# Hybrid decoder block: where the first tokens' last transposes of h stand, and what the second tokens' updates queue behind

## The chip, the cores and the metric

The kernel runs on one core of a Trainium2 chip. The metric is the time of one execution in microseconds (us) of device time, the median of several runs. The core has five engines that run side by side: TensorE (PE) for matmuls, VectorE (DVE) and ScalarE (ACT) for elementwise work, GpSimd (POOL), and SyncE (SP), which here issues the DMAs. Each engine runs its own list of instructions in order. Where an instruction needs what another engine makes, it waits for a semaphore. PE writes its products to PSUM, whose tiles here are 128 x 512 float32; ACT and DVE read them there.

## The reference

256 tokens of width 2048 go through one decoder block, in float32:

```
hn   = rms_norm(x, pre_mix_norm)
proj = hn @ w_in                         # pooling input, q, k, v
mixed = concat([pooling mixer, differential attention]) @ w_out
h    = x + rms_norm(mixed, post_mix_norm)
hn   = rms_norm(h, pre_ffn_norm)
ff   = (silu(hn @ w_gate) * (hn @ w_up)) @ w_down        # 2048 -> 5632 -> 2048
out  = h + rms_norm(ff, post_ffn_norm)
```

The change lies between `mixed` and the first block of `hn @ w_gate`.

## The kernel before, in words

A float32 product is made of three matmuls of rounded operands. Each operand is split into a high part (a copy by ACT) and a low part (value minus high part, by DVE), and high x high, low x high and high x low are summed in PSUM (lines 135, 136, 137). Weights come in by DMA on SP's queue, are split at lines 99 (ACT) and 100 (DVE), and are dropped when used.

The 256 tokens are two halves of 128, called first tokens (t = 0) and second tokens (t = 1). The token-major h is kept in `xn[0]` and `xn[1]`. The width 2048 is 16 blocks of 128, called k 0 to 15, and also four chunks c of four k each.

**Output projection** (`closing`, line 533). Four chunks of 512 output columns. In the last one (`gemm_a_skew`, line 149) the last twelve k are held, so that all matmuls of the first tokens end before those of the second tokens begin. Then, for each half: the sum of squares on ACT (540), the product with the gain on DVE (544), `rsqrt` (194), and the update h = x + mg * rs on DVE at line 567: four instructions of 512 columns for the first tokens, five for the second, whose first chunk is cut in two halves of 256.

**The transposes of h** (`h_parts(t, c)`, line 586). The next product needs h with k on the partitions. For one half t and one chunk c, PE transposes four blocks of `xn[t]` into one PSUM tile (590), named `tr` for c = 0 and 2 and `hs` for c = 1 and 3. Then for each of the four k, ACT writes the high part, scaled by the norm's gain (596), and DVE the low part (597). Both go into the tile `h` of that k, which holds the high and the low part of both halves. In the listings below `h_2305` is k 0 and `h_2320` is k 15; `xn_113` is the first tokens' h and `xn_114` the second tokens'.

**The first gate block** (`gemm_a_skew` on `w_g0`, line 618). Its first twelve k are held: all twelve for the first tokens, then all twelve for the second tokens, then k 12 to 15 for both in turn. The second matmul of each k (line 136) is the one that uses the low part of h.

**Where the transposes stand.** Two tables, `H_OUT` and `H_GATE` (lines 29 and 30), say behind which held matmuls a call of `h_parts` is written: key (half, n-th held k), value (t, c). `H_OUT` is for the last chunk of the output projection, `H_GATE` for the first gate block. `behind[0]` keeps later matmuls behind the last transpose written. Beyond such bounds (`tc.issue_after`) the order of each engine's list is chosen by a scheduler when the program is built. After the gate block come the sums of squares of h (`h_stats`, 601; each is kept behind the last high part by `behind_act`), the Silu of the gate (622), a copy of h to DRAM (626), and the pass over `w_u0` (662).

Of the kernel before, what the change touches and what calls it, by code (L numbers as in the profile page):

```python
# [8 lines left out]
F32 = mybir.dt.float32  # L9
# [3 lines left out]
ALU = mybir.AluOpType  # L13
# [12 lines left out]
RAW = 6  # L26
HOLD = 12

H_OUT = {(1, 6): (0, 0), (1, 8): (0, 1), (1, 10): (0, 2)}
H_GATE = {(0, 0): (0, 3), (0, 7): (1, 0), (0, 9): (1, 1), (0, 11): (1, 2), (1, 2): (1, 3)}  # L30
RING = 3
WINDOWS = (2, 4, 8, 16)
SK = (1, 3, 5)
# [12 lines left out]
def block_kernel(ctx: ExitStack, tc: tile.TileContext, x, xT, pos, cols, rows, lamv, invf, invcnt,  # L46
                 w_in, w_u, w_pool, w_out, w_g0, w_u0, w_gu, w_down, out):
    nc = tc.nc
    mm, act, dve, pool, sync = nc.tensor, nc.scalar, nc.vector, nc.gpsimd, nc.sync
# [10 lines left out]
    def nm(s):  # L60
        uid[0] += 1
        return f"{s}_{uid[0]}"

    def small(shape, dt=F32, tag="tiny", bufs=24):
        return tiny.tile(shape, dt, tag=tag, name=nm(tag), bufs=bufs)
# [4 lines left out]
    def bank2():  # L70
        return psum.tile([P, 512], F32, tag="tr", name=nm("tr"), bufs=2)
# [14 lines left out]
    def load_after(dst, src):  # L86

        with tc.issue_after(latest[0]):
            sync.dma_start(dst, src)
# [51 lines left out]
    def gemm_a(srcs, a, nk, order=None, before=lambda i: None):  # L141
        ps = [bank(), bank()]
        for i, k, wh, wl in a_steps(srcs, order):
            before(i)
            for t in range(2):
                mm_a(ps, a, t, k, wh, wl, i == 0, i == nk - 1)
        return ps

    def gemm_a_skew(srcs, a, nk, order, held_at, parts, hook):


        ps = [bank(), bank()]
        held = []
        for i, k, wh, wl in a_steps(srcs, order, held_at, parts):
            if i in held_at:
                held.append((i, k, wh, wl))
                if len(held) < len(held_at):
                    continue
                for t in range(2):
                    for n, (i, k, wh, wl) in enumerate(held):  # L160
                        mm_a(ps, a, t, k, wh, wl, i == 0, i == nk - 1)
                        hook(t, n)
                    behind[0] = last_mm[0]
                    if i == nk - 1:
                        yield t, ps[t]
            else:
                for t in range(2):
                    mm_a(ps, a, t, k, wh, wl, i == 0, i == nk - 1)
        if nk - 1 not in held_at:
            for t in range(2):  # L170
                yield t, ps[t]
# [17 lines left out]
    def variance(ss, scale, add=EPS):  # L189
        v = small([P, ss.shape[1]])  # L190
        dve.tensor_scalar(v, ss, scale, add, ALU.mult, ALU.add)
        return v

    def rsqrt(v):

        n = v.shape[1]
        r = small([P, n])
        act.activation(r, v, AF.Sqrt)
        y = small([P, n])
        dve.reciprocal(y, r)  # L200
        a = small([P, n])
        dve.scalar_tensor_tensor(a, y, -0.5, y, ALU.mult, ALU.mult)
        b = small([P, n])
        dve.tensor_tensor(b, a, v, ALU.mult)
        res = small([P, n])
        dve.scalar_tensor_tensor(res, b, 1.5, y, ALU.add, ALU.mult)
        return res
# [16 lines left out]
    g3 = lambda k: colt[:, 16 + k:17 + k]  # L224
# [50 lines left out]
    for k in range(NKD):  # L275
# [7 lines left out]
        for m in range(2):  # L283
            raw, hi, lo = raws[m]
            c = slice(j % 2 * 512, (j % 2 + n) * 512)
# [3 lines left out]
        for m in range(2):  # L289
            raw, hi, lo = raws[m]  # L290
            if n == 1 or j % 2 == 0:
                c = slice(j % 2 * 512, (j % 2 + n) * 512)
                act.activation(hi[:, c], raw[:, c], AF.Copy)
                dve.tensor_tensor(lo[:, c], raw[:, c], hi[:, c].bitcast(F32), ALU.subtract)
            c = slice(j % 2 * 512, (j % 2 + 1) * 512)
# [237 lines left out]
    def closing(srcs_of, a, nk, gains, order, tail, parts, hook, done):  # L533

        sst = small([P, 2, 4], tag="sst", bufs=2)
        mg = {}

        def square(c, t, ps):
            j2 = cp.tile([P, 512], mybir.dt.bfloat16, tag="sqj", name=nm("sqj"), bufs=2)
            act.activation(j2, ps, AF.Square, accum_out=sst[:, t, c:c + 1])  # L540

        def gained(c, t, ps):
            mg[c, t] = mg_tile()
            dve.tensor_tensor(mg[c, t], ps, gain, ALU.mult)

        for c in range(4):
            if c == 1:
                act.activation(small([P, 1]), sst[:, 0, 0:1], AF.Sqrt)
            gain = cp.tile([P, 512], F32, tag="gain", name=nm("gain"), bufs=2)
            load_after(gain, gains[c * 512:(c + 1) * 512].partition_broadcast(P))  # L550
            if c < 3:
                ps = gemm_a(srcs_of(c), a, nk, order, lambda i: before_k[0](c, i))
                for t in range(2):
                    square(c, t, ps[t][:, :])
                    gained(c, t, ps[t][:, :])
        pre = small([P, 2])
        dve.tensor_reduce(pre, sst[:, :, 0:3], AX.X, ALU.add)
        pre2 = small([P, 2])
        dve.tensor_scalar(pre2, pre, 1.0 / D, EPS, ALU.mult, ALU.add)
        for t, ps in gemm_a_skew(srcs_of(3), a, nk, order, range(nk - tail, nk), parts, hook):  # L560
            square(3, t, ps[:, :])
            v = variance(sst[:, t, 3:4], 1.0 / D, pre2[:, t:t + 1])
            gained(3, t, ps[:, :])
            rs = rsqrt(v)
            for c in range(4):
                for z in (slice(0, 256), slice(256, 512)) if c == 0 and t == 1 else (slice(0, 512),):
                    dve.scalar_tensor_tensor(h_c(c, t)[:, z], mg[c, t][:, z], rs, h_c(c, t)[:, z], ALU.mult, ALU.add)
                    done(c, t, z)

    m_k = (lambda k, t: mh[k // 2][:, k % 2, t * P:(t + 1) * P], lambda k, t: ml[k // 2][:, k % 2, t * P:(t + 1) * P])  # L570
    h_c = lambda c, t: xn[t][:, c * 512:(c + 1) * 512]
    h_act = parts_act("h")
# [13 lines left out]
    def h_parts(t, c):  # L586

        tr = bank2() if c % 2 == 0 else psum2.tile([P, 512], F32, tag="hs", name=nm("hs"), bufs=2)
        for j in range(4):
            last = mm.transpose(tr[:, j * P:(j + 1) * P], xn[t][:, (4 * c + j) * P:(4 * c + j + 1) * P], ident)  # L590
        behind[0] = last.ins
        for j in range(4):
            k = 4 * c + j
            o = tr[:, j * P:(j + 1) * P]
            hi, lo = (z(k)[:, t * P:(t + 1) * P] for z in (hh_k, hl_k))
            behind_act[0] = act.activation(hi, o, AF.Copy, scale=g3(k)).ins
            dve.scalar_tensor_tensor(lo, o, g3(k), hi.bitcast(F32), ALU.mult, ALU.subtract)

    behind_act = [None]

    def h_stats(t):
        for c in range(4):
            j2 = cp.tile([P, 512], mybir.dt.bfloat16, tag="sqj", name=nm("sqj"), bufs=2)
            with tc.issue_after(behind_act[0]):
                act.activation(j2, h_c(c, t), AF.Square, accum_out=ss3[:, t, c:c + 1])
        ss3s = small([P, 1])
        dve.tensor_reduce(ss3s, ss3[:, t, :], AX.X, ALU.add)
        dve.tensor_copy(rstd3[:, t:t + 1], rsqrt(variance(ss3s, 1.0 / D)))

    def h_hook(at):  # L610
        return lambda t, n: h_parts(*at[t, n]) if (t, n) in at else None

    closing(lambda c: [w_out[c, i] for i in range(4)], m_k, NKD, rows[0], (1, 2, 3, 0), HOLD, lambda i: (hold_parts,),
            h_hook(H_OUT), lambda c, t, z: None)

    a_h = (lambda k, t: hh_k(k)[:, t * P:(t + 1) * P], lambda k, t: hl_k(k)[:, t * P:(t + 1) * P])
    sg = []
    for t, ps in gemm_a_skew([w_g0[i] for i in range(4)], a_h, NKD, None, range(HOLD),
                             lambda i: (ring_parts if i < 2 * RING else hold_parts,), h_hook(H_GATE)):
        h_stats(t)  # L620
# [260 lines left out]
    def mg_tile():  # L881
        n = len(mgs)
        if used[0] == n:
            three = part("rh" if n % 2 == 0 else "rl", 3, F32)
            mgs.extend(three[:, i] for i in range(3))
        used[0] += 1
        return mgs[used[0] - 1]
# [5 lines left out]
    def store(c, t, z):  # L893
        sync.dma_start(out[t * P:(t + 1) * P, c * 512 + z.start:c * 512 + z.stop], h_c(c, t)[:, z])

    closing(lambda c: [w_down[c, i] for i in range(NF // 4)], f_k, NF, rows[1], None, 8,
            lambda i: (), lambda t, n: None, store)

# [57 lines left out]
```

## Time and profile before

| what | value |
|---|---|
| median of 3 runs | 1024.69 us (1024.68 to 1025.0) |
| the profiled execution's own time | 1026.65 us |
| its span, first to last instruction | 1024.8 us |
| PE busy | 1012.2 us, 99% of the span |
| DVE busy | 735.5 us, 72% |
| ACT busy | 539.5 us, 53% |
| DMA | 203.39 MB, mean 198 GB/s |

The profile is of one execution. In its timelines a row gives the start in us from the span's start, the length, the engine, the line, the operation, out<-in by the program's names without numbers, shapes, and the count; in brackets the time that the engine sat idle before it, and what released it. In the view of waits a row gives the engine and line that waited, whom it waited for, the sum in us, the number of waits and the longest. PE's instructions overlap: a matmul of 0.39 is followed by the next one after 0.23.

### The profile page before, as it was taken

The numbers are of one execution on the slowest core, as the hardware profiler recorded it, in microseconds if no ns is written. First come the engines' busy times: TensorE is split into PE (matmuls) and PEld (weight loads), VectorE is DVE, ScalarE is ACT, GpSimd is POOL, SyncE is SP. The second block draws the span as 40 slices with busy tenths as digits, with TensorE's granted clock in tenths as the row PEclk, the third lists the DMA queues.
The fourth block names the chain that finished last, engine by engine and source line by source line (L and its number), as shares of the span: only waits on it lengthen the run. The fifth ranks groups of instructions, "written<-read, shape, count | busy, mean of one in ns | idle before, by whom it ended". The sixth has DMA issues, their size and how long they took to land.

```text
span 1024.8 us, 12559 instructions
## 1 busy us (share of the span) xinstructions
PE 1012.2 (99%) x4787; PEld 841.7 (82%) x4787; DVE 735.5 (72%) x850; ACT 539.5 (53%) x643; POOL 28.4 (3%) x54
## 2 busy tenths in 40 slices
PE   9999999999999999999999999999999999999996
PEld 6889888988877888888888888888887888888885
DVE  6569755875677889898888988889887653454445
ACT  6666545654548555455454554645545553343332
POOL 0003300210000000000000000000000000000000
PEclk9999999999999999999999999999999999999999
DMA  9753555456774465555655556556565575556552
GB/s 337 284 191 131 180 186 177 151 169 217 237 255 135 165 228 192 199 201 194 206 197 195 202 185 205 206 201 200 174 211 189 196 287 198 191 196 216 181 189 82
DMA packets 57373, 203.39 MB, mean 198 GB/s; under 512 B 6880, under 2 KB 7520, under 8 KB 56544
## 3 DMA queue, kind: packets, MB, share of 16 engines
q1 hardware_dynamic: 57024, 202.44, 57.4%
q8 instruction: 37, 0.61, 0.2%
q14 instruction: 24, 0.20, 0.1%
q10 hardware_dynamic: 288, 0.15, 0.1%
HBM read 198.37 MB, written 4.19 MB: 198 GB/s over the span
## 4 chain that ended last, share of the span: by engine, by line
PE 98%; DVE 1%; DMA 0%; ACT 0%; issue 0%; DVEq 0%; SPq 0%; ACTq 0%
PE mm L136 16%; PE mm L137 16%; PE mm L135 16%; PE mm L768 9%; PE mm L769 9%; PE mm L770 9%; PE tr L770 3%; PE tr L769 3%; PE tr L768 3%; PE mm L174 2%; PE mm L175 2%; PE mm L176 2%; PE m L768 1%; PE m L769 1%; PE m L770 1%; PE m L692 1%
## 5 line engine op out<-in xcount | busy, mean ns | idle before, releaser
L100 DVE TENSOR_TENSOR wl<-raw,wh 128x1024 fp32r<-128x1024 f32 x88 | 104.7, 1222 | 107.6 <-ACT wh L99 107.6
L100 DVE TENSOR_TENSOR wlo<-raw,whi 128x1024 fp32r<-128x1024 f32 x89 | 110.5, 1241 | 61.9 <-ACT whi L99 56.5
L99 ACT ACTIVATE wh<-raw 128x1024 fp32r<-128x1024 f32 x88 | 89.3, 1052 | 122.4 <-PE mm L136 118.8
L678 DVE TENSOR_TENSOR wl<-raw,wh 128x2048 fp32r<-128x2048 f32 x50 | 114.6, 2292 | 44.0 <-ACT wh L674 43.7
L136 PE MATMUL mm<-wh,gl 128*128 128x512 f32 x352 | 137.3, 390 | 1.1 <-DVE gl L758 1.1
L674 ACT ACTIVATE wh<-raw 128x2048 fp32r<-128x2048 f32 x50 | 95.9, 1918 | 79.5 <-PE tr L769 56.4
L135 PE MATMUL mm<-wh,gh 128*128 128x512 f32 x352 | 134.9, 390 | 0.0
L137 PE MATMUL mm<-wl,gh 128*128 128x512 f32 x352 | 131.0, 389 | 0.0
L768 PE MATMUL mm<-wh,h 128*128 128x512 f32 x330 | 129.2, 392 | 0.0
L99 ACT ACTIVATE whi<-raw 128x1024 fp32r<-128x1024 f32 x89 | 94.0, 1056 | 65.7 <-PE mm L136 49.9
L769 PE MATMUL mm<-wh,h 128*128 128x512 f32 x330 | 128.5, 389 | 0.0
L770 PE MATMUL mm<-wl,h 128*128 128x512 f32 x330 | 128.4, 389 | 0.0
L674 ACT ACTIVATE wh<-T 128x2048 fp32r<-128x2048 f32 x30 | 57.6, 1920 | 73.8 <-DVE T L678 73.4
L136 PEld LDWEIGHTS mm<-wh,gl 128*128 128x128 f32 x352 | 66.1, 188 | 15.1 <-DVE gl L758 1.6
L137 PEld LDWEIGHTS mm<-wl,gh 128*128 128x128 f32 x352 | 66.1, 188 | 13.7
L135 PEld LDWEIGHTS mm<-wh,gh 128*128 128x128 f32 x352 | 66.0, 188 | 13.6
L678 DVE TENSOR_TENSOR wl<-T,wh 128x2048 fp32r<-128x2048 f32 x30 | 68.7, 2290 | 8.0 <-ACT wh L674 8.0
L770 PEld LDWEIGHTS mm<-wl,h 128*128 128x128 f32 x330 | 62.0, 188 | 12.9
L768 PEld LDWEIGHTS mm<-wh,h 128*128 128x128 f32 x330 | 62.0, 188 | 12.7
L769 PEld LDWEIGHTS mm<-wh,h 128*128 128x128 f32 x330 | 62.0, 188 | 12.5
L135 PE MATMUL mm<-whi,x 128*128 128x512 f32 x160 | 62.9, 395 | 0.6 <-ACT x L255 0.6
L136 PE MATMUL mm<-whi,x 128*128 128x512 f32 x160 | 62.8, 394 | 0.0
(246 smaller groups left out, 1941.3 us busy)
## 6 DMA issues: line engine op xcount, KB each, us to landing
raw<-in_w_gu SPq DMA_DIRECT2D x160, 512.0 KB, 4.2
raw<-in_w_down SPq DMA_DIRECT2D x88, 512.0 KB, 4.1
raw<-in_w_in SPq DMA_DIRECT2D x46, 512.0 KB, 3.8
raw<-in_w_out SPq DMA_DIRECT2D x32, 512.0 KB, 4.2
raw<-in_w_u SPq DMA_DIRECT2D x24, 512.0 KB, 3.7
raw<-in_w_g SPq DMA_DIRECT2D x8, 512.0 KB, 6.1
xn<-in_x SPq DMA_DIRECT2D x2, 1024.0 KB, 10.1
gain<-in_rows SPq DMA_DIRECT2D x8, 256.0 KB, 4.6
```

What stands on the lines that cost most here:

```text
L99: last_split[0] = act.activation(hi, raw, AF.Copy).ins
L100: (by or dve).tensor_tensor(lo, raw, hi.bitcast(F32), ALU.subtract)
L135: mm.matmul(ps[t][:, :], lhsT=a[0](k, t), rhs=wh, start=first, stop=False)
L136: mm.matmul(ps[t][:, :], lhsT=a[1](k, t), rhs=wh, start=False, stop=False)
L137: last_mm[0] = mm.matmul(ps[t][:, :], lhsT=a[0](k, t), rhs=wl, start=False, stop=last).ins
L174: mm.matmul(o, lhsT=wh, rhs=xh, start=st, stop=False)
L175: mm.matmul(o, lhsT=wh, rhs=xl, start=False, stop=False)
L674: put("act", lambda: act.activation(out_, in_, func, **kw))
L678: put("dve", lambda: dve.tensor_tensor(out_, a, b, op))
L768: put("mm", lambda: mm.matmul(o, lhsT=a[0], rhs=wh, start=first, stop=False))
L769: put("mm", lambda: mm.matmul(o, lhsT=a[1], rhs=wh, start=False, stop=False))
L770: put("mm", lambda: mm.matmul(o, lhsT=a[0], rhs=wl, start=False, stop=last))
```

## The change

```diff
-H_OUT = {(1, 6): (0, 0), (1, 8): (0, 1), (1, 10): (0, 2)}
-H_GATE = {(0, 0): (0, 3), (0, 7): (1, 0), (0, 9): (1, 1), (0, 11): (1, 2), (1, 2): (1, 3)}
+H_OUT = {(1, 6): (0, 0), (1, 8): (0, 1), (1, 10): (0, 2), (1, 11): (0, 3)}
+H_GATE = {(0, 7): (1, 0), (0, 9): (1, 1), (0, 11): (1, 2), (1, 2): (1, 3)}
...
             for c in range(4):
                 for z in (slice(0, 256), slice(256, 512)) if c == 0 and t == 1 else (slice(0, 512),):
-                    dve.scalar_tensor_tensor(h_c(c, t)[:, z], mg[c, t][:, z], rs, h_c(c, t)[:, z], ALU.mult, ALU.add)
+                    with tc.issue_after(behind_dve[0]) if behind_dve[0] is not None and t == 1 else nullcontext():
+                        dve.scalar_tensor_tensor(h_c(c, t)[:, z], mg[c, t][:, z], rs, h_c(c, t)[:, z], ALU.mult, ALU.add)
                     done(c, t, z)
 
+    behind_dve = [None]
...
             behind_act[0] = act.activation(hi, o, AF.Copy, scale=g3(k)).ins
-            dve.scalar_tensor_tensor(lo, o, g3(k), hi.bitcast(F32), ALU.mult, ALU.subtract)
+            behind_dve[0] = dve.scalar_tensor_tensor(lo, o, g3(k), hi.bitcast(F32), ALU.mult, ALU.subtract).ins
```

The call `h_parts(0, 3)`, which transposes k 12 to 15 of the first tokens, is written behind the last held matmul of the output projection instead of behind the first held k of the gate block. The low part that was written last is kept in `behind_dve`, and the five updates of the second tokens are placed behind it in DVE's list. When those updates are written, that is the low part of k 15 of the first tokens. The instructions and their number stay the same. Lines behind the change are two higher: 590, 596 and 597 become 592, 598 and 599, and 567 becomes 568.

On DVE, at the end of the output projection, there stood before (low parts are the rows that write `h`, updates those that write `xn_114`):

```order
L597 SCALAR_TENSOR_TENSOR h_2309<-hs_2978,colt,h_2309 128x128
L567 SCALAR_TENSOR_TENSOR xn_114<-mg_2486,tiny_3027,xn_114 128x256 x2
L567 SCALAR_TENSOR_TENSOR xn_114<-mg_2644,tiny_3027,xn_114 128x512
L567 SCALAR_TENSOR_TENSOR xn_114<-mg_2800,tiny_3027,xn_114 128x512
L567 SCALAR_TENSOR_TENSOR xn_114<-mg_3017,tiny_3027,xn_114 128x512
L597 SCALAR_TENSOR_TENSOR h_2310<-hs_2978,colt,h_2310 128x128
L597 SCALAR_TENSOR_TENSOR h_2305<-tr_3109,colt,h_2305 128x128
L597 SCALAR_TENSOR_TENSOR h_2311<-hs_2978,colt,h_2311 128x128
L597 SCALAR_TENSOR_TENSOR h_2306<-tr_3109,colt,h_2306 128x128
```

Now there stands, from the same low part of k 4 on (the last low part of the first tokens is that of k 15, `h_2320`):

```order
L599 SCALAR_TENSOR_TENSOR h_2309<-hs_2978,colt,h_2309 128x128
L599 SCALAR_TENSOR_TENSOR h_2310<-hs_2978,colt,h_2310 128x128
L599 SCALAR_TENSOR_TENSOR h_2311<-hs_2978,colt,h_2311 128x128
L599 SCALAR_TENSOR_TENSOR h_2312<-hs_2978,colt,h_2312 128x128
L599 SCALAR_TENSOR_TENSOR h_2313<-tr_2997,colt,h_2313 128x128
...
L599 SCALAR_TENSOR_TENSOR h_2319<-hs_3013,colt,h_2319 128x128
L599 SCALAR_TENSOR_TENSOR h_2320<-hs_3013,colt,h_2320 128x128
L568 SCALAR_TENSOR_TENSOR xn_114<-mg_2486,tiny_3040,xn_114 128x256 x2
L568 SCALAR_TENSOR_TENSOR xn_114<-mg_2644,tiny_3040,xn_114 128x512
L568 SCALAR_TENSOR_TENSOR xn_114<-mg_2800,tiny_3040,xn_114 128x512
L568 SCALAR_TENSOR_TENSOR xn_114<-mg_3030,tiny_3040,xn_114 128x512
L599 SCALAR_TENSOR_TENSOR h_2305<-tr_3109,colt,h_2305 128x128
```

The updates moved from behind the low part of k 4 to behind that of k 15, eleven low parts later. The second tokens' low parts, which alternated with the first tokens', now all come behind the updates. ACT's list of high parts moved in the same way.

On PE, in the gate block of the first tokens, there stood before (`tr_3109` is the second tokens' first group of transposes; `mm_3034` is the gate's PSUM tile of the first tokens):

```order
L137 MATMUL mm_3034<-wlo_3053,h_2309 128x512
L590 MATMUL tr_3109<-ident,xn_114 128x128 x2
L135 MATMUL mm_3034<-whi_3052,h_2310 128x512
L590 MATMUL tr_3109<-ident,xn_114 128x128 x2
L136 MATMUL mm_3034<-whi_3052,h_2310 128x512
```

And now, where the same PSUM tile is called `mm_3047`:

```order
L137 MATMUL mm_3047<-wlo_3066,h_2310 128x512
L135 MATMUL mm_3047<-hhi_3069,h_2311 128x512
L136 MATMUL mm_3047<-hhi_3069,h_2311 128x512
L137 MATMUL mm_3047<-hlo_3070,h_2311 128x512
L135 MATMUL mm_3047<-hhi_3069,h_2312 128x512
L136 MATMUL mm_3047<-hhi_3069,h_2312 128x512
L137 MATMUL mm_3047<-hlo_3070,h_2312 128x512
L592 MATMUL tr_3109<-ident,xn_114 128x128 x4
L135 MATMUL mm_3047<-hhi_3077,h_2313 128x512
```

The group moved from behind k 4 to behind k 7. Two more of the second tokens' groups moved back too: that of c = 1 from within k 8 to behind k 9, and that of c = 2 from behind k 9 into the first k of the second tokens.

The moved group of the first tokens' last four k, between output projection and gate block on PE, stood before and stands now (`mm_2809` is the output projection's tile):

```order
L137 MATMUL mm_2809<-hlo_2879,mh_563 128x512
L135 MATMUL mm_3034<-whi_3040,h_2305 128x512
L590 MATMUL hs_3075<-ident,xn_113 128x128 x4
L136 MATMUL mm_3034<-whi_3040,h_2305 128x512
L137 MATMUL mm_3034<-wlo_3041,h_2305 128x512
```

```order
L137 MATMUL mm_2809<-hlo_2879,mh_563 128x512
L135 MATMUL mm_3047<-whi_3053,h_2305 128x512
L592 MATMUL hs_3013<-ident,xn_113 128x128 x4
L136 MATMUL mm_3047<-whi_3053,h_2305 128x512
L137 MATMUL mm_3047<-wlo_3054,h_2305 128x512
```

In PE's list it did not move: before and now it stands behind the first matmul of the gate block. SP's list of DMAs is the same in both.

## The prediction

> **What bounds the kernel now.** I read the page first: how the engines share the span, and the chain that ended last.
>
> ```profile
> span 1024.8 us, 12559 instructions
> PE 1012.2 (99%) x4787; PEld 841.7 (82%) x4787; DVE 735.5 (72%) x850; ACT 539.5 (53%) x643; POOL 28.4 (3%) x54
> PE 98%; DVE 1%; DMA 0%; ACT 0%; issue 0%; DVEq 0%; SPq 0%; ACTq 0%
> ```
>
> TensorE (PE) is the path: 98% of the chain is its own matmuls. So nothing is won unless PE waits less, and every microsecond that PE waits anew is lost, unless a later wait of PE shrinks by it. Next the view of waits, PE's rows:
>
> ```profile
> PE tr L250 <- DVE warm L246: 1.5, 1, 1.5
> PE mm L136 <- DVE h L597: 1.3, 1, 1.3
> PE mm L136 <- DVE gl L758: 1.1, 1, 1.1
> PE mm L135 <- ACT x L255: 0.6, 1, 0.6
> ```
>
> Four waits, 4.5 us together. The second is the one in reach: a gate matmul waits 1.3 us for a low part of h^T that VectorE (DVE) writes at line 597. The third follows the gate/up stage, which PE itself feeds, so it moves along with PE and takes up nothing. Then PE's timeline around the second wait (start, length, instruction):
>
> ```profile
> 285.02 0.39 PE L137 MATMUL mm<-hlo,mh 128*128 128x512 f32 x1
> ...
> 297.26 0.39 PE L137 MATMUL mm<-hlo,mh 128*128 128x512 f32 x1
> 297.50 0.60 PE L590 MATMUL tr<-ident,xn 128*128 128x128 f32 x4
> 297.85 0.48 PE L135 MATMUL mm<-hhi,mh 128*128 128x512 f32 x1
> 298.16 0.40 PE L136 MATMUL mm<-hhi,ml 128*128 128x512 f32 x1
> ...
> 306.20 0.40 PE L137 MATMUL mm<-wlo,h 128*128 128x512 f32 x1
> 306.43 0.38 PE L590 MATMUL tr<-ident,xn 128*128 128x128 f32 x2
> 306.57 0.48 PE L135 MATMUL mm<-whi,h 128*128 128x512 f32 x1
> 306.89 0.38 PE L590 MATMUL tr<-ident,xn 128*128 128x128 f32 x2
> 308.54 0.50 PE L136 MATMUL mm<-whi,h 128*128 128x512 f32 x1 [1.27 <-DVE h L597]
> ...
> 314.35 0.40 PE L135 MATMUL mm<-whi,h 128*128 128x512 f32 x1
> ...
> 328.46 0.39 PE L135 MATMUL mm<-whi,h 128*128 128x512 f32 x1
> ```
>
> From 285.02 to 297.26 are 54 equal steps of matmuls: 12.24/54 = 0.227 us a matmul. A group of four transposes adds 0.45: from 297.26 to 298.16 are 0.90, and two matmuls would be 0.45. At 308.54 k 5 of the first tokens (k counted from 0; tile h_2310) gets its low part. At 314.35 the second tokens' gate matmuls begin, at 328.46 the pass over w_u0.
>
> Why that low part is late stands in ScalarE's (ACT) and DVE's timelines; each k needs a high part from ACT (L596), then a low one from DVE (L597):
>
> ```profile
> 305.48 0.37 ACT L596 ACTIVATE h<-hs,colt 128x128 fp32r<-128x128 f32 x1 [0.49 <-DVE h L597]
> 308.52 0.37 ACT L596 ACTIVATE h<-hs,colt 128x128 fp32r<-128x128 f32 x1 [0.84 <-DVE h L597]
> 309.31 0.37 ACT L596 ACTIVATE h<-hs,colt 128x128 fp32r<-128x128 f32 x1 [0.16 <-DVE h L597]
> ```
>
> ```profile
> 305.36 2.86 DVE L567 SCALAR_TENSOR_TENSOR xn<-mg,tiny,xn 128x256 f32<-128x256 f32 x5
> 308.14 0.35 DVE L597 SCALAR_TENSOR_TENSOR h<-hs,colt,h 128x128 fp32r<-128x128 f32 x1
> 308.92 0.35 DVE L597 SCALAR_TENSOR_TENSOR h<-hs,colt,h 128x128 fp32r<-128x128 f32 x1 [0.18 <-ACT h L596]
> 309.71 0.35 DVE L597 SCALAR_TENSOR_TENSOR h<-hs,colt,h 128x128 fp32r<-128x128 f32 x1 [0.18 <-ACT h L596]
> 309.98 0.60 DVE L597 SCALAR_TENSOR_TENSOR h<-tr,colt,h 128x128 fp32r<-128x128 f32 x2
> ```
>
> The high part of k 5 starts at 305.48, but its low part stands behind the five updates of the second tokens (2.86 us) and starts at 308.14. The other thing to see is the beat. Low part 308.92, next high part 309.31, next low part 309.71: within one PSUM tile each step waits for the other engine, 0.79 us a part. Where the next part is of another tile it follows in 0.27 (309.71 to 309.98). Before the change the two tokens' parts alternate between tiles, which hides half of that beat.
>
> **The change part by part.** *The moved transposes* cost and bring nothing on PE. In PE's row the group of the first tokens' last four k stands where it stood, behind the first gate matmul. Only its place in the program's text moves, and with it what the updates queue behind: the low part of k 15 instead of k 11.
>
> *The updates behind the parts* is the whole effect. What goes: the 1.27 us wait, since the low part of k 5 no longer has updates ahead. It starts 0.40 after its high part (308.52 to 308.92), at 305.88. What comes: the second tokens' first transposes read updated x and so need the first update; that now stands on DVE behind ten more low parts, k 6 to k 15. In PE's row those transposes stand after k 7, and the matmuls run in the row's order: behind them wait the gate matmuls of k 8 to 15 and all else.
>
> The clock of that wait. Low parts start: k 6 at 306.67, k 7 at 307.46 (0.79 each), k 8 in a new tile at 307.73, k 11 at 310.10, k 12 in a new tile at 310.37, k 15 at 312.74. The updates follow 0.27 later, at 313.01. The durations of an update are in the row of its line (minimum, median, maximum):
>
> ```profile
> L567 DVE SCALAR_TENSOR_TENSOR xn<-mg,tiny,xn x5: 477/747/747, 305.4 to 307.5; 128x512 f32<-128x512 f32 x3, 128x256 f32<-128x256 f32 x2
> ```
>
> The first half update (0.48) ends at 313.49, and PE starts 0.05 later (308.14 + 0.35 = 308.49 against 308.54), at 313.54. When is PE there? Without the two transposes its slot at 306.43 takes k 5, and nine matmuls of k 5 to 7 last till 306.43 + 9 x 0.227 = 308.47; their low parts end at 306.23, 307.02 and 307.81, ahead of the second matmul of each k (306.66, 307.34, 308.02). So PE stands still from 308.47 to 313.54: **5.07 us**. The second pair of transposes needs the second half update. Five updates in 2.86, with the full ones (2.86 - 0.75)/4 = 0.53 apart on the mean, the half ones nearer 0.40: it ends near 313.89, and the matmul of k 8 starts about 0.14 after it (306.43 to 306.57) and the 0.05, at 314.08.
>
> From there to the pass over w_u0 stand 12 matmuls of the first tokens, 36 and 24 of both, and three groups of transposes: 72 x 0.227 + 3 x 0.45 + 0.08 (after a group a matmul takes 0.31 and not 0.227) = 17.8, so 331.9 instead of 328.46. That is **+3.4 us**: 5.07 + 0.4 of waits in, and 1.27 with some 0.8 of small gaps around it out (the 0.8 is what is left by difference). The same count on the trace of before, 314.35 + 60 x 0.227 + 0.45 = 328.4, meets 328.46.
>
> *What hides the rest.* The second tokens' own parts now begin after the last update, at 313.01 + 2.86 = 315.9, with PE there at 314.08 + 12 x 0.227 + 0.5 = 317.3. They are alone, so they go at 0.79, three of four, and 0.27: 0.66 a part, against PE's 0.68 a k. It holds, with little over. Behind them stand on ACT the squares and the weights of w_u0:
>
> ```profile
> 321.57 0.37 ACT L596 ACTIVATE h<-hs,colt 128x128 fp32r<-128x128 f32 x1 [1.03 <-DVE h L597]
> 332.25 1.05 ACT L99 ACTIVATE whi<-raw 128x1024 fp32r<-128x1024 f32 x1
> ```
>
> ```profile
> 321.98 0.35 DVE L597 SCALAR_TENSOR_TENSOR h<-hs,colt,h 128x128 fp32r<-128x128 f32 x1 [0.44 <-ACT h L596]
> 333.33 1.22 DVE L100 TENSOR_TENSOR wlo<-raw,whi 128x1024 fp32r<-128x1024 f32 x1 [0.40 <-ACT whi L99]
> ```
>
> Sixteen second parts take 10.6, so the last starts near 315.9 + 10.3 = 326.2, or 329.6 if the three weight splits of DVE among them (1.14 apart) all come on top: 4.2 to 7.6 later than 321.98. The split of w_u0's k 6 and 7 then ends that much after 334.55. PE needs it at 328.46 + 36 x 0.227 + 0.45 = 337.1, plus 3.4. Its 2.5 us of cover become 1.7 at best and -1.7 at worst. I take no loss, because parts and splits overlap between two engines, and keep 1.7 for the range. On SP the copy of the second tokens' x to DRAM waits for the updates, at about 316 instead of 308.25; the four weight loads behind it wait till 318.10 as it is:
>
> ```profile
> 308.25 0.33 SPq L89 DMA_DIRECT2D kept<-xn  x1
> 318.10 10.79 SPq L83 DMA_DIRECT2D raw<-in_w_u  x4
> ```
>
> They wait for splits to free their buffers, not for it, so it costs nothing.
>
> *A wait this long.* No row of before has PE idle over 1.5 us. After the 1.27 us the matmuls go on at their usual step, so by the rows the sum stays at +3.4. But the start of the span shows that PE has a slower step:
>
> ```profile
> 1.45 4.02 PE L250 MATMUL tr<-warm 128*128 128x512 bf16 x9 [1.45 <-DVE warm L246]
> 7.47 0.63 PE L136 MATMUL mm<-whi,x 128*128 128x512 f32 x1
> 7.90 0.63 PE L137 MATMUL mm<-wlo,x 128*128 128x512 f32 x1
> 10.46 0.51 PE L136 MATMUL sc<-whi,x 128*128 128x512 f32 x1
> 10.81 0.40 PE L137 MATMUL sc<-wlo,x 128*128 128x512 f32 x1
> ```
>
> Matmuls there are 0.43 apart (7.47 to 7.90), and only from 10.5 on near 0.227. If 5 us of rest brings that state back, each slow microsecond loses 1 - 0.227/0.43 = 0.47. How long it lasts is bounded by none and by the 9.0 us from 1.45 to 10.46: 0 to 4.2 us. I take none in the sum, as the only rest in mid-kernel brought none. The Trainium skill, "TensorE: Matmul & The Clock Gate", Part 1, speaks against this change here: it says that the array falls to half clock after an idle window of about 3.4 us, on a window that runs freely, and returns after a busy one. By that rule a rest of 5 us contains a whole window in about half of all runs, and the estimate would be 1.6 to 3.2 us more. The trace agrees on the two rates (0.43 and 0.227), and no run here shows a rest that long.
>
> **The rivals.**
>
> *The slow step comes back after the rest.* For it: the start shows 0.43. Against it: the longest rest of before is too short to tell. Price from rows: the slow matmuls behind the warm-up run from 1.45 + 4.02 = 5.47 to 10.46, 5.0 us, so 5.0 x 0.47 = 2.3 on top: 1030.4, at most 1028.1 + 4.2 = 1032.3. The Trainium skill's page above is why I give it as much as 0.35.
>
> *The weights of w_u0 come late.* Price up to 1.7, about 0.8: 1028.9, with a new wait of PE at L137 about 340. Chance 0.08.
>
> *No slower: the beat is shorter than I think.* If ACT ran ahead of DVE, parts would follow at 0.27. Then k 15 starts at 305.88 + 10 x 0.27 = 308.58 and not 312.74: PE waits 0.9 instead of 5.07, and 3.4 - 4.16 gives -0.8, 1023.9. It decides at (6.86 - 3.4)/10 = 0.35 a part. For it: DVE alone does two in 0.60. Against it: ACT's rows wait for DVE at 308.52 and 309.31. Chance 0.07, 0.02 of it for more than 0.2%, if the removed gaps were worth more too.
>
> That the change does nothing at all is excluded by the order; its first half does nothing on PE, as said.
>
> **How the numbers follow.** The profiled execution took 1026.65 for a span of 1024.8; the runs' median is 1024.69. The difference lies outside these engines' work, so I add +3.4 to the median: 1024.69 + 3.4 = **1028.1**, chance 0.50. A measurement here can tell about 0.2%, 2.05 us, from no change; above 1026.7 is slower. The forecast, the slow step and the late weights are all beyond it: 0.50 + 0.35 + 0.08 = 0.93. Same 0.05, faster 0.02. The range goes from 1027.4 (0.7 less, if the beat is 0.07 shorter in ten parts) to 1031.2, which takes in the late weights and half of the slow step's upper end.
>
> **What would show it.** Right: PE's wait of about 5 us at the transposes of the second tokens, released by the update; none at h of k 5; low parts 0.79 apart between 305.9 and 312.7; the second tokens' gate matmuls from about 317.3, w_u0 from about 331.9. The slow step would show as matmuls 0.43 apart after the wait. Wrong: PE released at the transposes before 311, or a wait elsewhere that gives the loss back.

## The result: slower by 0.66%, more than was forecast

| kernel | median us (range, runs) | ratio to before [95% interval] |
|---|---|---|
| before | 1025.47 (1024.68 to 1027.33, 6) | |
| changed | 1032.78 (1030.61 to 1035.67, 6) | 1.0066 [1.0054, 1.0078] |

The forecast was 1028.1 with a range up to 1031.2; the median lies 1.6 above that end. The sign was right; the loss is 5.5 to 8.0 us by the interval, where 3.4 were forecast. The profiled execution after took 1035.67 us for a span of 1033.9.

### The profile page after: what moved, and what is told of

It is laid out like the page before. It is cut to its first block, busy times and chain, and to the rows that moved or that the text cites. A ratio compares the mean times of both kernels' runs of the same rounds, so it can differ in the third digit from the quotient of the medians.

```text
span 1033.9 us, 12559 instructions
## 1 busy us (share of the span) xinstructions
PE 1015.4 (98%) x4787; PEld 843.4 (82%) x4787; DVE 736.1 (71%) x850; ACT 539.4 (52%) x643; POOL 28.5 (3%) x54
## 4 chain that ended last, share of the span: by engine, by line
PE 93%; DVE 3%; ACT 1%; DMA 1%; issue 1%; DVEq 0%; SPq 0%; ACTq 0%
PE mm L135 14%; PE mm L137 14%; PE mm L136 14%; PE mm L770 9%; PE mm L772 9%; PE mm L771 9%; PE tr L772 3%; PE tr L770 3%; PE tr L771 3%; PE mm L174 2%; PE mm L175 2%; PE mm L176 1%; PE m L772 1%; PE m L770 1%; PE m L771 1%; DMA raw<-in_w_out 1%
```

## The profile after

The head of the page after, and its chain of work that ended last:

```profile
span 1033.9 us, 12559 instructions
PE 1015.4 (98%) x4787; PEld 843.4 (82%) x4787; DVE 736.1 (71%) x850; ACT 539.4 (52%) x643; POOL 28.5 (3%) x54
...
PE 93%; DVE 3%; ACT 1%; DMA 1%; issue 1%; DVEq 0%; SPq 0%; ACTq 0%
```

The instructions are the same in number. PE held 98% of the chain before and holds 93% now. The chain leaves PE in three places: from 267 to 285 for weights of the output projection, which is ahead of the change and costs PE a wait of only 0.3; from 305 to 316 over the parts and the update; and from 341 to 362 over weight splits and `gg`, DVE's products of the gate and the up half. So only a part of the five points belongs to the change. PE is also busy 3.2 us longer (1015.4 against 1012.2) with the same work, so part of its work went slower. The view of waits, PE's rows (total, times, longest):

```profile
PE tr L592 <- DVE xn L568: 4.8, 1, 4.8
PE mm L135 <- ACT x L255: 1.8, 1, 1.8
PE tr L250 <- DVE warm L246: 1.5, 1, 1.5
PE mm L136 <- DVE gl L760: 1.1, 1, 1.1
PE mm L770 <- DVE gg L685: 0.7, 1, 0.7
PE mm L137 <- DVE wlo L100: 0.3, 1, 0.3
```

The wait for h of 1.3 us is gone. The first row is the new wait that was forecast; the one for `gg` was not forecast. The second is an old one at the span's start, 0.6 before, and the last lies ahead of the change, at 285.43. PE's timeline from the first gate matmul on:

```profile
305.09 0.39 PE L135 MATMUL mm<-whi,h 128*128 128x512 f32 x1
...
311.07 0.40 PE L137 MATMUL mm<-hlo,h 128*128 128x512 f32 x1
316.29 1.11 PE L592 MATMUL tr<-ident,xn 128*128 128x128 f32 x4 [4.83 <-DVE xn L568]
...
317.63 0.63 PE L136 MATMUL mm<-hhi,h 128*128 128x512 f32 x1
318.06 0.63 PE L137 MATMUL mm<-hlo,h 128*128 128x512 f32 x1
...
320.81 0.39 PE L136 MATMUL mm<-hhi,h 128*128 128x512 f32 x1
321.04 0.39 PE L137 MATMUL mm<-hlo,h 128*128 128x512 f32 x1
...
336.49 0.39 PE L135 MATMUL mm<-whi,h 128*128 128x512 f32 x1
...
358.25 0.39 PE L770 MATMUL mm<-wh,h 128*128 128x512 f32 x1
...
361.87 0.50 PE L770 MATMUL mm<-wh,h 128*128 128x512 f32 x1 [0.74 <-DVE gg L685]
```

Behind the wait the matmuls are 0.43 apart (317.63 to 318.06) and take 0.63 instead of 0.39. From 320.8 on they are 0.23 apart again. The windows of PE show the granted clock of those stretches, as a share of PE's full clock (columns: stretch and its length, busy time and instructions, granted clock, DMA share, GB/s):

```profile
313.50:314.00 0.50, 0.00 (x0) 0.69 0.00 0
314.00:314.50 0.50, 0.00 (x0) 0.50 0.00 0
316.00:318.00 2.00, 1.71 (x6) 0.50 0.00 0
...
320.00:320.50 0.50, 0.50 (x5) 0.50 1.10 459
320.50:321.00 0.50, 0.50 (x4) 0.98 0.82 328
```

The clock falls to half at 313.69 (a mean of 0.69 from 313.5 to 314.0 is 0.38 of that stretch at full clock, 0.19 us), 2.2 us after the last matmul's end (311.07 + 0.40), and comes back at 320.51: 6.82 us. Of these, 4.22 lie on work (316.29 to 320.51).

The cause of the wait is in DVE's timeline, the first tokens' low parts and the updates:

```profile
308.69 0.35 DVE L599 SCALAR_TENSOR_TENSOR h<-hs,colt,h 128x128 fp32r<-128x128 f32 x1 [0.43 <-ACT h L598]
...
310.26 0.35 DVE L599 SCALAR_TENSOR_TENSOR h<-hs,colt,h 128x128 fp32r<-128x128 f32 x1 [0.44 <-ACT h L598]
310.53 0.34 DVE L599 SCALAR_TENSOR_TENSOR h<-tr,colt,h 128x128 fp32r<-128x128 f32 x1
...
315.49 0.35 DVE L599 SCALAR_TENSOR_TENSOR h<-hs,colt,h 128x128 fp32r<-128x128 f32 x1 [0.43 <-ACT h L598]
315.76 0.87 DVE L568 SCALAR_TENSOR_TENSOR xn<-mg,tiny,xn 128x256 f32<-128x256 f32 x2
```

The beat is 0.79 within a PSUM tile (308.69 to 310.26 are two steps) and 0.27 across (310.26 to 310.53), as read from before, and the updates come 0.27 behind the last part.

Where the time came from is best seen by stretch, since one profiled execution and the next differ by some us ahead of the change (below). The same marks stand in PE's timeline of before:

```profile
302.29 0.39 PE L135 MATMUL mm<-whi,h 128*128 128x512 f32 x1
...
350.22 0.39 PE L768 MATMUL mm<-wh,h 128*128 128x512 f32 x1
```

The pass over w_u0 takes 21.76 in both (328.46 to 350.22, and 336.49 to 358.25). So there are three stretches: the start, up to the first gate matmul; the gate block, from there to w_u0; and the rest, from the first gate/up matmul to the span's end.

| us | start | gate block | w_u0 | rest | span |
|---|---|---|---|---|---|
| before | 302.29 | 26.17 | 21.76 | 674.58 | 1024.8 |
| changed | 305.09 | 31.40 | 21.76 | 675.65 | 1033.9 |
| difference | 2.80 | 5.23 | 0 | 1.07 | 9.1 |

The change is made behind the start, so its own part is 5.23 + 1.07 = 6.3 us, of which the forecast had 3.4.

## The experiments

The theory after the result has three terms: the queue behind the parts costs the 3.4 of the forecast; the rest that it gives PE brings the half clock, 1.8; and behind w_u0 PE waits for `gg`, which costs 1.07. Rivals: the queue alone costs all of the 5.2; the half clock is no consequence of the rest; and the 1.07 is scatter. In the expectations the stretch behind w_u0 is counted from its last matmul, 0.23 us earlier than in the tables here.

| kernel | median us (range, runs) | ratio to before of the same call [95%] | start | gate block | rest |
|---|---|---|---|---|---|
| tables_only | 1025.76 (1024.46 to 1028.0, 11) | 0.9996 [0.9987, 1.0005] | 301.40 | 26.20 | 674.64 |
| queue_only | 1029.34 (1028.34 to 1032.28, 6) | 1.0037 [1.0023, 1.005] | 302.71 | 28.53 | 675.60 |
| rest_filled_18 | 1028.43 (1028.2 to 1029.4, 7) | 1.0026 [1.0015, 1.0037] | 300.66 | 29.61 | 674.57 |
| rest_filled_6 | 1033.39 (1031.56 to 1036.17, 6) | 1.0074 [1.0059, 1.0089] | 301.58 | 30.80 | 675.86 |
| rest_filled_15 | 1029.05 (1028.15 to 1029.83, 7) | 1.0027 [1.0016, 1.0038] | 302.08 | 29.60 | 674.56 |
| changed_again | 1033.14 (1031.03 to 1033.48, 5) | 1.0064 [1.0051, 1.0076] | 302.44 | 31.48 | 675.62 |
| squares_out | 1030.87 (1029.5 to 1031.78, 5) | 1.0047 [1.0034, 1.006] | 300.24 | 31.13 | 674.57 |
| changed_gated | 1031.82 (1030.1 to 1033.05, 5) | 1.0057 [1.0043, 1.007] | 300.60 | 31.39 | 674.55 |
| interleaved | 1026.3 (1024.53 to 1027.89, 11) | 0.9997 [0.9988, 1.0007] | 303.77 | 24.54 | 676.04 |
| before_gated | 1026.38 (1024.84 to 1028.77, 11) | 1.0 [0.9991, 1.0009] | 302.04 | 26.13 | 674.67 |
| interleaved_gated | 1024.22 (1023.07 to 1025.47, 8) | 0.9979 [0.9968, 0.999] | 300.40 | 24.55 | 674.59 |

### One part of the change alone

tables_only has the moved entry of the tables without the queue; queue_only has the queue on the old tables, so the updates stand behind the low part of k 11.

```
tables_only:
-H_OUT = {(1, 6): (0, 0), (1, 8): (0, 1), (1, 10): (0, 2)}
-H_GATE = {(0, 0): (0, 3), (0, 7): (1, 0), (0, 9): (1, 1), (0, 11): (1, 2), (1, 2): (1, 3)}
+H_OUT = {(1, 6): (0, 0), (1, 8): (0, 1), (1, 10): (0, 2), (1, 11): (0, 3)}
+H_GATE = {(0, 7): (1, 0), (0, 9): (1, 1), (0, 11): (1, 2), (1, 2): (1, 3)}

queue_only:
+                    with tc.issue_after(behind_dve[0]) if behind_dve[0] is not None and t == 1 else nullcontext():
+                        dve.scalar_tensor_tensor(h_c(c, t)[:, z], mg[c, t][:, z], rs, h_c(c, t)[:, z], ALU.mult, ALU.add)
...
+            behind_dve[0] = dve.scalar_tensor_tensor(lo, o, g3(k), hi.bitcast(F32), ALU.mult, ALU.subtract).ins
```

> Only the two tables are changed; the second tokens' updates are free as before. The lists of PE, DVE and ACT come out in the same order as before. All theories: no difference from before, within the scatter (under 0.1%, 1 us), PE's wait for h L597 again about 1.3 us. If it differs by more, the scatter between programs is larger than taken.

> Only the updates are queued; the tables are those of before, so the last low part written ahead of the updates is that of k 11 and not k 15: four parts less, 2.6 us. Theory A (a rest at the transposes, plus a clock drop when a window of 3.4 us is mostly idle): rest about 2.2 us, +0.8 us over before with no drop of the clock, +2.5 if it drops. Rival B (the excess of the change over +3.4 is late weights of w_u0 and what hangs on them): +0.8 and about 1 more at the pass over w_u0, whatever the clock does.

tables_only costs nothing: the moved transposes do not matter by themselves, as the prediction said. queue_only already loses 0.37%. PE's timeline of queue_only at the new wait, and its windows:

```profile
308.68 0.40 PE L137 MATMUL mm<-hlo,h 128*128 128x512 f32 x1
311.30 1.08 PE L592 MATMUL tr<-ident,xn 128*128 128x128 f32 x4 [2.23 <-DVE xn L568]
...
312.61 0.63 PE L136 MATMUL mm<-hhi,h 128*128 128x512 f32 x1
```

```profile
308.00:311.00 3.00, 1.08 (x5) 1.00 0.00 0
...
311.50:312.00 0.50, 0.50 (x4) 0.54 0.00 0
312.00:313.00 1.00, 1.00 (x4) 0.50 0.00 0
...
314.50:315.00 0.50, 0.50 (x4) 0.54 1.07 442
```

A rest of 2.23 us was enough for the half clock. It fell only at 311.54, when PE worked again, and lasted to 314.96, 3.42 us. So the four parts more that the moved entry puts ahead of the updates are not needed for the half clock, but they double the rest. By the stretches queue_only loses 2.36 in the gate block, of which 3.42 x 0.47 = 1.6 is the estimate for the half clock (worked out below), and 1.02 behind w_u0.

### The rest filled with work

Into PE's list, between the last matmul of k 7 and the second tokens' first transposes, go 18 warm-up matmuls (15 and 6 in the two others), whose product is not used. They take no time from the path, as PE waits there anyway.

```
+        if (t, c) == (1, 0):
+            with tc.issue_after(last_mm[0]):
+                for _ in range(18):
+                    mm.matmul(tr[:, :], lhsT=warm[:, 0:P], rhs=warm, start=True, stop=True)
```

> The change as it is, with 18 bf16 matmuls of ones into the idle PSUM tile of the second tokens' transposes, placed behind the matmuls of k 7 (results overwritten). They fill some 3.9 of the 4.8 us of rest; PE still resumes when the update is done. Theory A: granted clock stays at 1.00 at that place, matmuls 0.23 apart right after, about 2 us less than the changed kernel, +4 to +4.5 over before. Rival B: no less than the changed kernel. Rival C (the excess is scatter at the start of the span): no less than the changed kernel in the stretch from the last output projection to w_u0.

> As the kernel with 18, but with 6 such matmuls, 1.3 us, so the rest is about 3.5 us, hardly over one window of 3.4 us. If the clock drops whenever a window is mostly idle: still drops in most runs, time as the changed kernel, 0 to -1 us. If a whole window must be idle: it nearly never drops, -2 us as with 18.

> As the kernels with 18 and 6 filling matmuls, with 15: rest about 1.6 us. By the drops seen at rests of 2.2, 3.5 and 4.8 us and none at 0.9 and 1.3, the limit lies between. If less than about half of a window idle is enough: drops in some executions, +1.6 us in those. If not: clock as before, time as with 18.

rest_filled_18, PE's timeline at the fill (of the 18, 17 are in the trace), and then rest_filled_6's first transposes behind its fill:

```profile
307.12 3.83 PE L594 MATMUL tr<-warm 128*128 128x512 bf16 x17
311.86 0.83 PE L596 MATMUL tr<-ident,xn 128*128 128x128 f32 x4 [0.91 <-DVE xn L568]
```

```profile
312.78 1.12 PE L596 MATMUL tr<-ident,xn 128*128 128x128 f32 x4 [3.54 <-DVE xn L568]
```

rest_filled_15, the windows around its rest of 1.6 us:

```profile
312.00:313.00 1.00, 0.00 (x0) 1.00 0.00 0
313.00:314.00 1.00, 0.70 (x5) 1.00 0.00 0
314.00:315.00 1.00, 1.00 (x7) 1.00 0.00 0
```

With the rest cut to 0.9 or 1.6 us the clock stays full, and the gate block takes 29.6: 3.43 over before, the forecast's 3.4. With 6 matmuls PE rests 3.54, the clock falls for 3.4 us, of which 2.95 are on work, and the gate block takes 30.80. So the half clock follows the rest, and its price in the changed kernel is 31.40 - 29.60 = 1.8. The count from the rows agrees nearly: 4.22 us of slow work lose 1 - 0.227/0.427 = 0.47 each, 2.0. One thing differs besides the fill: with 15 and 18 matmuls the scheduler also orders the second tokens' parts and some weight splits of ACT and DVE otherwise; with 6 their order is that of the changed kernel. Taking 0.47 of the slow work off gives a gate block of 29.4 for the kernel with 6 (30.80 - 1.38) and for the changed one (31.40 - 1.98), so by this estimate that difference is worth about 0.2.

With 15 and 18 the wait for `gg` is gone as well (rest 674.56 and 674.57). So rest_filled_18 comes out 0.26% over before, 2.7 us, where 4 to 4.5 were expected. The median of rest_filled_6 is no lower than that of the changed kernel (1.0074 and 1.0066, with intervals that overlap); its stretches put it 0.4 lower.

### The late release behind w_u0

squares_out leaves six of the eight squares of h out on ACT. changed_gated moves the two `gated` products (they make `gg`), which free the PSUM tiles that the fifth group of gate/up products writes next, ahead of the 1.75 us low part `rl` on DVE.

```
squares_out:
-        for c in range(4):
+        for c in range(1):
...
-        dve.tensor_reduce(ss3s, ss3[:, t, :], AX.X, ALU.add)
-        dve.tensor_copy(rstd3[:, t:t + 1], rsqrt(variance(ss3s, 1.0 / D)))
+        dve.tensor_reduce(ss3s, ss3[:, t, 0:1], AX.X, ALU.add)
+        dve.tensor_copy(rstd3[:, t:t + 1], rsqrt(variance(ss3s, 4.0 / D)))

changed_gated:
     first_stage(1)
+    gg = [gated(ps[t][:, :], t) for t in range(2)]
     raw_stage(1)
-    gg = [gated(ps[t][:, :], t) for t in range(2)]
```

> The changed kernel as it is, for comparison on this chip and for the granted clock of more executions. Theory A (the clock drops whenever a window of 3.4 us is mostly idle, so at a rest of 4.8 us always): +5.5 to +7.5 over before, mean granted clock of every execution 0.002 to 0.003 under that of before, one stretch of 3.4 or 6.8 us at 0.50 behind the rest. If only a wholly idle window does it: no drop in about half of the executions, and these near +4.

> The changed kernel without six of the eight sums of squares of h (the norm is taken from the first 512 columns of each half), 3.7 us less on ACT ahead of the weights of w_u0 and the Silu. If late ACT work is what makes PE wait at the first product behind w_u0 (gg, 0.7 us, and 1.1 us in the stretch from there to the end): that wait goes, stretch from w_u0's end to the span's end as before (674.8), 1 us less than the changed kernel. If that loss comes from elsewhere: the same as the changed kernel. The rest at the transposes and the clock stay as in the changed kernel.

> The changed kernel with the same two gated products moved ahead of rl, nothing else. Theory A: the 0.7 us wait for them goes and the part behind w_u0 is 674.8 instead of 675.9, so about 1.1 us less than the changed kernel: a ratio near 1.0055 to before. The wait at the second tokens' transposes (4.8) and the slow matmuls behind it stay. Theory B: the loss moves to another wait behind w_u0, ratio 1.0065 as the changed kernel.

changed_again repeats the result: 1.0064, with 675.62 for the rest, so the 1.07 is no scatter. In both experiments the wait for `gg` is gone and the rest is that of before (674.57 and 674.55); the gate block keeps its long wait and its half clock (31.13 and 31.39). DVE's rows of the two kernels, before and then after, say why:

```profile
349.99 1.75 DVE L678 TENSOR_TENSOR rl<-raw,rh 128x1536 fp32r<-128x1536 f32 x1
351.65 1.40 DVE L683 SCALAR_TENSOR_TENSOR gg<-mm,rstd,sg 128x512 f32<-128x512 f32 x2
```

```profile
359.40 1.75 DVE L680 TENSOR_TENSOR rl<-raw,rh 128x1536 fp32r<-128x1536 f32 x1
361.07 1.41 DVE L685 SCALAR_TENSOR_TENSOR gg<-mm,rstd,sg 128x512 f32<-128x512 f32 x2
```

PE needs the first of these tiles 12 matmuls after the first gate/up product: 12 x 0.227 = 2.72. Before, `gg` starts 1.43 behind that product (351.65 - 350.22), and its first half, 0.7, ends in time. After, it starts 2.82 behind it (361.07 - 358.25) and ends 0.8 late. So DVE is 1.4 us later against PE than before. That the squares are part of the chain that makes it late is shown. Whether the queue alone would make it late without the half clock is not: the wait for `gg` comes with every half clock among the kernels that keep all squares and the old place of `gated` (queue_only, rest_filled_6, changed_again) and is absent in rest_filled_15 and 18, whose order on ACT and DVE differs too. In interleaved, below, the wait comes at full clock.

### A kernel with the gain and without the wait

The change takes away a wait of 1.27 for a low part that stood behind five updates. interleaved, made from the kernel before, puts neither all updates nor all parts first: on DVE the first tokens' parts of k 4 to 11 alternate with the updates, one or two after each. interleaved_gated has the two `gated` products ahead of `rl` as well, and before_gated has only that.

```
+MIX = (1, 2, 1, 2)
...
+            if t == 1 and later:
+                later.pop(0)()
             for c in range(4):
...
+                    if later and t == 1:
+                        chain[0] = u.ins
+                        for _ in range(MIX[c]):
+                            later.pop(0)()
...
+            def both(hi=hi, lo=lo, o=o, k=k):
+                behind_act[0] = act.activation(hi, o, AF.Copy, scale=g3(k)).ins
+                with tc.issue_after(chain[0]) if late and chain[0] is not None else nullcontext():
+                    n = dve.scalar_tensor_tensor(lo, o, g3(k), hi.bitcast(F32), ALU.mult, ALU.subtract)
...
+            late = (t, c) in ((0, 1), (0, 2))
+            later.append(both) if late else both()
```

> From the kernel before: the low parts of k 5 to 11 of the first tokens and the five updates stand in turn on DVE (k 4, half update, k 5, half update, k 6, update, k 7, k 8, update, k 9, update, k 10, k 11), each update in the 0.44 us in which DVE waits for ACT anyway. Theory A: the wait of 1.27 us for h and the small gaps around it go, no new wait at the transposes; the stretch of the gate block 1.5 to 1.9 us shorter, -1.5 to -1.9 us over before, clock as before. If the beat between ACT and DVE were not what binds, an update would push each part back by its full 0.67 us and PE would wait as long as before: no change.

> The kernel before with the same two gated products moved ahead of rl, nothing else. The kernel before has no wait for them, so by both theories the time is that of before, within 0.05%: ratio 1.000, the gate block 26.2 and the part behind w_u0 674.8. A gain here would mean that interleaved_gated's gain, if any, is not the interleaving's.

> Interleaved, and behind the pass over w_u0 the two gated products (they free the two PSUM banks that the fifth group of products writes) stand on VectorE ahead of the low part of the second pair's blocks (rl, 1.66 us) instead of behind it. Theory A (the 1.65 us that interleaving wins are given back only because these banks are freed late): the first gated product starts near 351.6 instead of 353.3 on interleaved's clock, TensorE's wait of 1.1 us for it goes, the part behind w_u0 is 674.8 again instead of 676.3, and the time is 1.5 us below before: 1024.5 beside 1026.1 of before, a ratio near 0.9985. Theory B (VectorE is late by a whole split there, and whatever stands last is waited for): TensorE then waits about as long for rl or for the split after it, and the ratio is 1.000.

interleaved wins the gate block (24.54 against 26.17, no wait for h, none at the transposes) and gives it back behind w_u0 (676.04). So the 1.5 to 1.9 less that were expected came in the gate block, but not in the time (0.9997). Its rows there, `gg` on DVE and then the wait on PE:

```profile
353.29 1.40 DVE L699 SCALAR_TENSOR_TENSOR gg<-mm,rstd,sg 128x512 f32<-128x512 f32 x2
```

```profile
354.09 0.50 PE L784 MATMUL mm<-wh,h 128*128 128x512 f32 x1 [1.14 <-DVE gg L699]
```

interleaved_gated has DVE's two instructions in the other order, and these are all of PE's waits in it:

```profile
348.27 1.41 DVE L699 SCALAR_TENSOR_TENSOR gg<-mm,rstd,sg 128x512 f32<-128x512 f32 x2
349.59 1.75 DVE L694 TENSOR_TENSOR rl<-raw,rh 128x1536 fp32r<-128x1536 f32 x1
```

```profile
PE tr L251 <- DVE warm L247: 1.5, 1, 1.5
PE mm L137 <- DVE gl L774: 1.1, 1, 1.1
PE mm L136 <- ACT x L256: 1.0, 1, 1.0
```

The rest is 674.59 again, the gate block stays at 24.55, and the kernel is faster than before by 0.21% (0.1 to 0.3), where 1.62/1025 = 0.16% was to be had by the stretches. before_gated gains nothing, so the moved products are worth something only where PE would wait for them. This version beats both kernels.

## Why the prediction was wrong

Its mechanism and its main term were right. The moved transposes cost nothing (tables_only). The wait at the second tokens' first transposes is 4.83, forecast 5.07. The beat is 0.79 in a tile and 0.27 across. The sum of the gate block without the half clock is 3.43, forecast 3.4 (rest_filled_15 and 18). There is no wait for h.

Two terms that it set to nothing were not nothing.

- *A wait this long*: the step that failed is "I take none in the sum, as the only rest in mid-kernel brought none". The only rest of before was 1.27, and the runs show that rests of 0.9, 1.27 and 1.6 bring no half clock while 2.2, 3.5 and 4.8 do. A row of a short rest said nothing on a long one. All six kernels that rest 2.2 us or more (the changed one, changed_again, changed_gated, squares_out, queue_only, rest_filled_6) fell to half in their profiled execution. The four with the full rest of 4.8 also have a mean granted clock of 0.994 to 0.996 in all 21 timed runs, where the kernels without half clock have 0.997 to 0.999 in all runs but one (0.996). So at the rest of this change it was no matter of chance; for rests of 2.2 and 3.5 the timed runs (0.994 to 0.997) do not settle how often. The price named for this rival, 2.3, was near: it measured 1.8. It had a chance of 0.35 and should have been the likeliest case. The Trainium skill, "TensorE: Matmul & The Clock Gate", Part 1, asks for an idle window of about 3.4 us; the measured rest of 2.23 was shorter than that and still had its half clock. Here the measurement decides: the half of all runs that the prediction made of the rule was too few.
- *What hides the rest*: "I take no loss, because parts and splits overlap between two engines" held for the weights of w_u0, the place that was named: that pass takes 21.76 in both. But the prediction followed the delayed work only to the first place where PE meets it. The squares and the splits behind them came later too, and DVE reached `gg` 1.4 us later against PE: 1.07 lost at the gate/up products. The third wait of before that the prediction passed over as PE's own was another one (`gl`, 1.1 in both).

With both the sum is 3.4 + 1.8 + 1.1 = 6.3, and 1024.69 + 6.3 = 1031.0, inside the range's end. The medians differ by 7.3, with an interval of 5.5 to 8.0, and the second measurement by 0.51% to 0.76%; the 6.3 lie within both. The remainder of 1.0 up to the medians is not settled. The median of before that the prediction started from, 1024.69, was lower than those taken since (medians of 1025.47 to 1026.54); beside the result it is 0.8 lower. These 0.8 and 1.0 are what carries the measured 1032.78 from 1031.0 over the range's end.

The rival with the other sign, parts that follow at 0.27, is refuted by the beat.

## What to carry to other kernels

When an order moves work behind a queue, follow the delayed engine beyond the first place where the critical engine meets it, down to the last buffer it frees: here the second such place cost 1.07. In these runs a rest of the matmul engine of 2.2 us or more cost more than its length, about 0.47 us for each us of work in the 3.4 or 6.8 us of half clock; work whose product nobody needs, put in the rest, took that off. Where two kinds of work stand before one another, alternating them can keep both in time (24.5 against 26.2 and 31.4 in the gate block), and its gain shows only when the next wait is removed as well.

## What the runs showed of the hardware that was not expected

- The half clock came with rests of 2.23, 3.54 and 4.83 us and not with 0.91, 1.27 or 1.59. In the profiled executions it lasted 3.4 us (queue_only, rest_filled_6, squares_out) or 6.8 (changed, changed_again, changed_gated). It fell 2.2 to 5.1 us after the last matmul's end, in queue_only and squares_out only after PE had begun to work again.
- The start of the span differs between executions of code that is the same there: the first gate matmul comes at 300.24 to 305.09. In the profiled execution after, 1.8 us (0.6 before) went on the first wait for x. Its slow matmuls at the start, 0.42 apart, went on to 13.35, where they ended near 10.5 before, though the granted clock of the profile's rows shows full speed there (1.00 from 7 to 14 us in both). A row of x2 holds two matmuls: the first row below is two slow ones, the second two at the usual 0.23.

```profile
12.51 1.00 PE L135 MATMUL mm<-whi,x 128*128 128x512 f32 x2
13.35 0.63 PE L136 MATMUL mm<-whi,x 128*128 128x512 f32 x2
13.81 0.39 PE L135 MATMUL sc<-whi,x 128*128 128x512 f32 x1
```
